# Cross attention in a decoder step: three heads' softmax ahead of the sample rows', two PSUM banks in turn for the heads' logits, and other banks for the first feed-forward block

## The chip, the core and the metric

The kernel runs on one core of a Trainium2 chip. The metric is the device time of one execution in microseconds (us); the time before is the median of three runs. Five engines work side by side, each through a queue of its own in a fixed order: TensorE (PE, with its weight loads as PEld), VectorE (DVE), ScalarE (ACT), GpSimd (POOL) and SyncE (SP), which issues most DMA transfers. An instruction that waits for a semaphore holds up everything that is queued behind it on its engine.

## The reference, cut to what matters

One layer of a hybrid decoder is computed in fp32 for 256 prompt tokens and 8 sample tokens (T = 264 columns): a mixer of sliding-window attention and a state-space scan, then cross attention into 256 memory tokens, then a feed-forward network with a short convolution. The change lies in the cross attention and in the first block of the feed-forward network:

```python
def cross_attend(x, mem_k, mem_v, g_cross, w_cq, cq_norm_g, w_co):
    q = rms_norm((rms_norm(x, g_cross) @ w_cq).reshape(b, t, MEM_HEADS, MEM_HEAD_DIM), cq_norm_g)
    logits = jnp.einsum('bqhd,bshd->bhqs', q, mem_k) * MEM_HEAD_DIM ** -0.5
    p = jax.nn.softmax(logits, axis=-1)
    o = jnp.einsum('bhqs,bshd->bqhd', p, mem_v)
    return o.reshape(b, t, D_XATTN) @ w_co

def conv_ffn(x, past, g_ffn, w_up, conv_w, conv_b, w_down):
    u, new_past = causal_dwconv(rms_norm(x, g_ffn) @ w_up, past, conv_w, conv_b)
    gate, val = jnp.split(u, 2, axis=-1)
    return (jax.nn.silu(gate) * val) @ w_down, new_past
```

There are 4 heads of 128 channels. The prompt's memory keys and values are computed here from the memory tokens; each sample token has its own cached keys and values, which are loaded.

## The kernel before, in words

**Weights.** A product of full precision is made of three matmuls (mm3, L104 to L106): the activations and the weights are split into a high and a low part. A weight part of 128 x 1024 is loaded on SP's queue (wraw, L83), cast on ACT to its high part (whi, L89), and the rest is made on DVE (wlo, L90); each of the three has 4 buffers. mm3 needs whi and wlo.

**PSUM.** There are eight banks of 128 x 512: three called "mm", two "t", and one each of "s", "x" and "y". A bank can be written anew only when everything that reads it is done.

**Order.** The code is traced in the order of its lines, and a scheduler then sets the order on each engine by a model of the times, with a higher priority for weights and for some evacuations (tc.high_priority), and with tc.issue_after for some groups of matmuls. So the order within an engine is fixed before the kernel runs, and an edit in the order of the code can move instructions that it doesn't touch.

**Cross attention**, from about 540 to 620 us of the profiled execution. The queries and the keys stand in SBUF (qk). Then, in the code's order:

- sample_probs (L1134 to L1172): the logits of the 8 sample rows, 32 matmuls against the loaded keys kt (L1144) into bank x; the rows' scale sst with a sum of squares in bank y (L1154), a square root on ACT (L287, called from rms) and two small DVE instructions (L1157, L1159); a maximum and its scaled negative (L1160, L1161); exp (L1163), reciprocal and scale (L1164, L1165); two transposes (L283) and two copies (L1172).
- probs(h) for each of the 4 heads of the prompt (L1194 to L1214): two pairs of fp32 matmuls for the logits into bank s (L1198; the profile counts four for two instructions), the maximum (L1201), a small multiply (L1202), two exps with their sums (L1206), the reciprocal (L1207), two scales (L1209), four transposes into a bank t (L283) and one copy to SBUF (L1214).
- v_pair(i), twice: the memory values of two heads, by mm3 with weights w_cv into two banks mm; two evacuations by ACT (vp<-mm, L1230).
- sample_out after the first v_pair: 16 matmuls of 128 x 512 into bank x (L1180), four DVE instructions (rs, L1183 and L1185), a transpose into bank y, and two splits (L97) that read it, one for each half of the rows.
- out_head(h) (L1236): two matmul pairs, into bank y for heads 0 and 2 and into bank s for heads 1 and 3, and a split of the result into ohl (L97: a cast on ACT, a subtraction on DVE).
- the output projection with w_co, by mm3 from ohl into two banks mm and two banks t, then x2_ev (L1285), which adds the residual (res) and splits the sum into x2h and x2l.

**The feed-forward network** starts at 619.91 us with proj of L1374: two units of up-projection per block i, in the two banks t or two banks mm in turn; block 0 takes banks mm, as the last steps of the output projection do.

Functions on ACT that need another table (square root, exp, silu) are preceded by an ACT_TABLE_LOAD, which the build puts in where the order on ACT asks for it. The names in the orders below end in the number of the buffer's use: e_7276 is the exp of head 1, e_7258 that of head 0, kt_7217 to kt_7223 are sample keys, y_7481 is the transpose of sample_out, y_7487 and s_7626 are the outputs of heads 0 and 3, sst_7243 is the sample rows' scale.

## Time and profile before

| what | us |
| --- | --- |
| median of three runs | 1385.63 (1385.51 to 1386.66) |
| the profiled execution's own time | 1386.54 |
| its span in the trace | 1384.3 |
| PE busy | 1376.5 (99%) |
| DVE, ACT, POOL busy | 1048.7, 766.1, 94.8 |
| DMA moved | 298.31 MB, 215 GB/s |

The profiled execution is 0.9 us above the median, and 2.24 us of it lie outside the span. A timeline row has start, duration, engine, line and operation, output<-inputs, shapes, how many instructions were put together, and in brackets how long the engine stood idle before and whose end it waited for. PE's instructions overlap, so the gap from start to start is what one costs, and the duration of a row is longer. L1198 x4 stands for one head's logits, L283 x4 for one head's transposes, L1144 x32 for one of the two groups of the sample rows' logits.

### The profile page before, as it was taken

How to read it: one execution, taken by the hardware profiler on the slowest of the kernel's cores; microseconds unless marked ns; L12 is line 12 of the kernel's file. 1: busy time of each engine (PE TensorE's matmuls, PEld its weight loads, DVE VectorE, ACT ScalarE, POOL GpSimd, SP SyncE). 2: the span in 40 equal slices, each digit the busy share in tenths (PEclk: the TensorE clock that was granted, in tenths of full speed). 3: DMA queues.
4: the chain of work that ended last, by engine and by line, in shares of the span. 5: the costliest groups of instructions: out<-in, count | busy, mean ns of one | idle time of the engine just before them, and what ended most of it. 6: DMA issues, size and time to landing. Idle time of an engine off the chain costs nothing.

```text
span 1384.3 us, 28768 instructions
## 1 busy us (share of the span) xinstructions
PE 1376.5 (99%) x11415; PEld 1348.3 (97%) x11415; DVE 1048.7 (76%) x1865; ACT 766.1 (55%) x1261; POOL 94.8 (7%) x286
## 2 busy tenths in 40 slices
PE   9999999999999999999999999999999999999999
PEld 8999999999999999889999999999999999999998
DVE  7979799999987774478777775777577757765655
ACT  7667755556545555476565544554455445543532
POOL 0000011111000000002010000000000000000000
PEclk9999999999999999999999999999999999999999
DMA  7954467777677566766576765676667656655664
GB/s 296 331 163 135 145 209 254 232 245 259 234 220 239 182 240 211 308 219 193 187 256 216 259 210 188 214 255 214 186 214 244 196 185 198 198 183 185 192 188 139
DMA packets 89477, 298.31 MB, mean 215 GB/s; under 512 B 12032, under 2 KB 17152, under 8 KB 88832
## 3 DMA queue, kind: packets, MB, share of 16 engines
q1 hardware_dynamic: 83840, 277.61, 60.6%
q0 software_dynamic: 5504, 18.88, 4.2%
q8 instruction: 89, 1.46, 0.4%
q14 instruction: 44, 0.36, 0.1%
HBM read 280.77 MB, written 16.23 MB: 215 GB/s over the span
## 4 chain that ended last, share of the span: by engine, by line
PE 97%; DMA 1%; DVE 1%; ACT 0%; issue 0%; SPq 0%; ACTq 0%
PE mm L105 21%; PE mm L104 20%; PE mm L106 20%; PE t L105 10%; PE t L106 9%; PE t L104 9%; PE t L245 1%; PE t L283 1%; PE y L830 1%; DMA wraw<-in_w_co_dram 1%; PE y L846 0%; DMA open<-in_open_dram 0%; PE x L283 0%; DVE wlo L90 0%; PE s L245 0%; PE mm L245 0%
## 5 line engine op out<-in xcount | busy, mean ns | idle before, releaser
L89 ACT CAST whi<-wraw 128x1024 fp32r<-128x1024 f32 x440 | 459.5, 1047 | 518.2 <-PE mm L105 278.3
L90 DVE TENSOR_TENSOR wlo<-wraw,whi 128x1024 fp32r<-128x1024 f32 x440 | 540.7, 1231 | 220.8 <-ACT whi L89 214.9
L105 PE MATMUL t<-x2l,whi 128*128 128x264 f32 x704 | 200.6, 285 | 0.0
L105 PE MATMUL mm<-x2l,whi 128*128 128x264 f32 x704 | 200.5, 285 | 0.0
L105 PE MATMUL mm<-hl,whi 128*128 128x264 f32 x704 | 199.6, 285 | 0.0
L106 PE MATMUL t<-x2h,wlo 128*128 128x264 f32 x704 | 199.1, 283 | 0.0
L106 PE MATMUL mm<-x2h,wlo 128*128 128x264 f32 x704 | 198.7, 283 | 0.0
L106 PE MATMUL mm<-hh,wlo 128*128 128x264 f32 x704 | 197.6, 282 | 0.0
L104 PE MATMUL mm<-x2h,whi 128*128 128x264 f32 x704 | 196.5, 279 | 0.4 <-DVE res L1285 0.4
L104 PE MATMUL t<-x2h,whi 128*128 128x264 f32 x704 | 196.4, 279 | 0.0
L104 PE MATMUL mm<-hh,whi 128*128 128x264 f32 x704 | 194.1, 280 | 0.0
L104 PE MATMUL mm<-xh,whi 128*128 128x264 f32 x576 | 163.8, 286 | 0.0
L105 PE MATMUL mm<-xl,whi 128*128 128x264 f32 x576 | 163.5, 285 | 0.0
L106 PE MATMUL mm<-xh,wlo 128*128 128x264 f32 x576 | 162.1, 286 | 0.0
L104 PEld LDWEIGHTS mm<-x2h,whi 128*128 128x128 f32 x704 | 132.3, 188 | 0.6 <-ACT whi L89 0.6
L104 PEld LDWEIGHTS t<-x2h,whi 128*128 128x128 f32 x704 | 132.3, 188 | 0.0
L106 PEld LDWEIGHTS t<-x2h,wlo 128*128 128x128 f32 x704 | 132.1, 188 | 0.0
L106 PEld LDWEIGHTS mm<-x2h,wlo 128*128 128x128 f32 x704 | 132.1, 188 | 0.0
L106 PEld LDWEIGHTS mm<-hh,wlo 128*128 128x128 f32 x704 | 131.9, 188 | 0.0
L105 PEld LDWEIGHTS mm<-hl,whi 128*128 128x128 f32 x704 | 131.7, 187 | 0.0
L105 PEld LDWEIGHTS mm<-x2l,whi 128*128 128x128 f32 x704 | 131.7, 187 | 0.0
L105 PEld LDWEIGHTS t<-x2l,whi 128*128 128x128 f32 x704 | 131.7, 187 | 0.0
(497 smaller groups left out, 2893.8 us busy)
## 6 DMA issues: line engine op xcount, KB each, us to landing
wraw<-in_w_up_dram SPq DMA_DIRECT2D x176, 512.0 KB, 4.4
wraw<-in_w_in_dram SPq DMA_DIRECT2D x96, 512.0 KB, 4.7
wraw<-in_w_dn_dram SPq DMA_DIRECT2D x88, 512.0 KB, 4.4
wraw<-in_w_out_dram SPq DMA_DIRECT2D x48, 512.0 KB, 4.3
h<-in_h_dram POOLq DMA_DIRECT2D x32, 256.0 KB, 4.6
hn<-in_h_dram SPq DMA_DIRECT2D x16, 512.0 KB, 4.8
out_state_s_dram<-hn POOLq DMA_DIRECT2D x16, 512.0 KB, 3.6
e<-dram_la SPq DMA_DIRECT2D x16, 256.0 KB, 4.8
```

Source lines behind the costliest of these rows:

```text
L89: S.copy(out=hi, in_=x)
L90: V.tensor_tensor(out=lo, in0=x, in1=hi.bitcast(F32), op=ALU.subtract)
L104: PE.matmul(out, wh, xh, start=start, stop=False)
L105: PE.matmul(out, wh, xl, start=False, stop=False)
L106: return PE.matmul(out, wl, xh, start=False, stop=stop)
L245: PE.matmul(first[c][:, :T], pre[k // 2][i][:, k % 2, c * 128:(c + 1) * 128], A[k // 8][x][:, k % 8, :], start=k + i + x == 0, stop=k == K ...
L283: return PE.transpose(out, in_, cst[0:k, C_ID:C_ID + k])
L830: PE.matmul(y[o:o + 64, (h // 2) * 128:(h // 2) * 128 + 128], xdt[:, h, :], es[h // 4][:, h % 4, :], start=True, stop=True)
```

## The change

sample_probs is cut into three functions: sample_logits (the matmuls), sample_scale (the sum of squares, the square root and the two multiplies) and sample_probs (maximum to transposes). The calls stand in another order: sample_logits, sample_scale, the last loads of the sample values, probs of heads 0, 1 and 2, sample_probs, probs of head 3. The logits of heads 1 and 3 go to bank y, those of heads 0 and 2 to bank s as before. The first up-projection block takes banks s and x, in place of two banks mm. From L1155 on, lines move by 7, and from L1269 on by 8: L1198 becomes L1205, L1206 becomes L1213, L1214 L1221, L1230 L1237, L1236 L1243, L1374 L1382; L1144 stays.

```diff
-    def sample_probs():
+    def sample_logits():
         lg = psum("x")
...
+        return lg
+
+    def sample_scale():
         p = psum("y")
         PE.matmul(p[:, 0:1], qq.rearrange("p m b -> p (m b)"), ones[:, 0:1], start=True, stop=True)
         st = xp.tile([128, 4], F32, name="sst")
-        fs, mx, den = st[:, 0:1], st[:, 1:2], st[:, 2:3]
+        fs = st[:, 0:1]
         V.tensor_tensor(out=fs, in0=p[:, 0:1], in1=r1s[:, 1:2], op=ALU.mult)
         rms(fs, fs, 128)
         V.tensor_tensor(out=fs, in0=fs, in1=r1s[:, 0:1], op=ALU.mult)
+        return st
+
+    def sample_probs(lg, st):
+        fs, mx, den = st[:, 0:1], st[:, 1:2], st[:, 2:3]
         V.tensor_reduce(out=mx, in_=lg[:, 0:256], op=ALU.max, axis=AX.X)
...
     def probs(h, f):
-        p = psum("s")
+        p = psum("y" if h % 2 else "s")
...
-    sample_probs()
+    lg = sample_logits()
+    sst = sample_scale()
     for b in range(6, 8):
...
-    for h in range(2):
+    for h in range(3):
         probs(h, fq[:, :, h])
-    for h in range(2, 4):
-        probs(h, fq[:, :, h])
+    sample_probs(lg, sst)
+    probs(3, fq[:, :, 3])
...
-            proj([w_up[2 * i], w_up[2 * i + 1]], X2, ev, tag="t" if i % 2 else "mm")
+            proj([w_up[2 * i], w_up[2 * i + 1]], X2, ev, tag=["s", "x"] if i == 0 else "t" if i % 2 else "mm")
```

The edit moves instructions on every engine. Two places matter here. The first is about the second group of the sample rows' logits (574 us in the trace of before).

On ACT, before: from the weight cast whi_7561 (565.26 us), over the square root of the sample rows' scale and the evacuations of the first v_pair (vp), to the exps, with the sample rows' exp (es) ahead of head 0's.

```order
L89 CAST whi_7561<-wraw_7559 128x1024
L287 ACTIVATE sst_7243<-sst_7243,eps_414 128x1
L1230 ACTIVATE vp_6702<-mm_7335,rmc_6139 128x256
L89 CAST whi_7567<-wraw_7565 128x1024
L1230 ACTIVATE vp_6702<-mm_7336,rmc_6139 128x256
L89 CAST whi_7643<-wraw_7641 128x1024
L89 CAST whi_7649<-wraw_7647 128x1024
L1163 ACT_TABLE_LOAD
L1163 ACTIVATE es_7250,sst_7243<-x_7192,sst_7243 128x256
L1206 ACTIVATE e_7269,st_7266<-s_7263,st_7266,fq_7174 128x256 x2
```

There is one table load in it. The same place now, from the same weight cast; e_7258 is head 0's exp, e_7276 head 1's, t_7264 head 0's transposes.

```order
L89 CAST whi_7561<-wraw_7559 128x1024
L1213 ACT_TABLE_LOAD
L1213 ACTIVATE e_7258,st_7255<-s_7252,st_7255,fq_7174 128x256 x2
L287 ACT_TABLE_LOAD
L287 ACTIVATE sst_7243<-sst_7243,eps_414 128x1
L1237 ACTIVATE vp_6702<-mm_7335,rmc_6139 128x256
L89 CAST whi_7567<-wraw_7565 128x1024
L1237 ACTIVATE vp_6702<-mm_7336,rmc_6139 128x256
L1213 ACT_TABLE_LOAD
L1213 ACTIVATE e_7276,st_7273<-y_7270,st_7273,fq_7174 128x256
L1221 COPY vp_6702<-t_7264 128x512
L1213 ACTIVATE e_7276,st_7273<-y_7270,st_7273,fq_7174 128x256
```

Head 0's exps now stand ahead of the square root, so there are three table loads, and the evacuations of the first v_pair and the cast whi_7567 stand between head 0's exps and head 1's.

On PE at the same place, before: the second group of the sample rows' logits (L1144) stands among the matmuls of the second v_pair (mm_7498).

```order
L104 MATMUL mm_7498<-whi_7561,mh1_5570 128x256
L105 MATMUL mm_7498<-wlo_7562,mh1_5570 128x256
L1144 MATMUL x_7192<-kt_7223,pp1_6703 32x256 x4
L1144 MATMUL x_7192<-kt_7217,pp1_6703 32x256 x4
L1144 MATMUL x_7192<-kt_7219,pp1_6703 32x256 x4
L1144 MATMUL x_7192<-kt_7221,pp1_6703 32x256 x4
L106 MATMUL mm_7498<-whi_7561,ml_6279 128x256
```

Of the second v_pair's matmuls, 53 stand ahead of that group. Now, with head 1's transposes (t_7282) and the logits of head 3 (y_7317) behind it:

```order
L106 MATMUL mm_7497<-whi_7507,ml_6128 128x256
L1144 MATMUL x_7192<-kt_7223,pp1_6703 32x256 x4
L1144 MATMUL x_7192<-kt_7217,pp1_6703 32x256 x4
L1144 MATMUL x_7192<-kt_7219,pp1_6703 32x256 x4
L1144 MATMUL x_7192<-kt_7221,pp1_6703 32x256 x4
L283 MATMUL t_7282<-cst_68,e_7276 128x128
L1205 MATMUL y_7317<-qk_6701 128x256 x2
L283 MATMUL t_7282<-cst_68,e_7276 128x128 x3
L104 MATMUL mm_7498<-whi_7507,mh0_5569 128x256
```

Here 33 of the second v_pair's matmuls stand ahead of the group; the logits of heads 1 and 2 and head 0's four transposes (t_7264) have moved ahead of it too.

The second place is the end of cross attention. On PE, before: the rows from head 2's logits (s_7299) to the first matmul of the output projection (mm_7637).

```order
L1198 MATMUL s_7299<-qk_6701 128x256 x2
L283 MATMUL t_7293<-cst_68,e_7287 128x128 x4
L283 MATMUL y_7481<-cst_68,rs_7476 128x128
L1198 MATMUL s_7317<-qk_6701 128x256 x2
L283 MATMUL t_7311<-cst_68,e_7305 128x128 x4
L1236 MATMUL y_7487<-vp_6702 128x256 x2
L1236 MATMUL s_7492<-vp_6702 128x256 x2
L104 MATMUL mm_7637<-ohl_7191,whi_7643 128x264
```

And now, from the second v_pair's last matmul on:

```order
L106 MATMUL mm_7498<-whi_7567,ml_6555 128x256
L1243 MATMUL s_7626<-pp1_6703,vp_6702 128x256
L283 MATMUL y_7481<-cst_68,rs_7476 128x128
L1243 MATMUL s_7626<-pp1_6703,vp_6702 128x256
L1243 MATMUL y_7487<-vp_6702 128x256 x2
L104 MATMUL mm_7637<-ohl_7191,whi_7643 128x264
```

The logits and transposes of the heads have moved up from here, and so has head 1's output (s_7492). Head 3's output (s_7626) stands right behind the second v_pair, and head 0's (y_7487) follows the sample rows' transpose (y_7481), which is in the same bank, with half of s_7626 between them.

On ACT at the same place, now; whi_7719 and whi_7725 are weight casts for w_co, and the two rows with y_7481 are the two splits of the sample rows.

```order
L1237 ACTIVATE vp_6702<-mm_7497,rmc_6139 128x256
L1237 ACTIVATE vp_6702<-mm_7498,rmc_6139 128x256
L97 CAST ohl_7191<-y_7481 128x4x4
L97 CAST ohl_7191<-s_7626 128x256
L89 CAST whi_7719<-wraw_7717 128x1024
L89 CAST whi_7725<-wraw_7723 128x1024
L97 CAST ohl_7191<-y_7481 128x4x4
L97 CAST ohl_7191<-y_7487 128x256
L97 CAST ohl_7191<-y_7621 128x256
```

Before, the two splits of y_7481 stood together (x2 in one row), ahead of every cast for w_co but two; now head 3's cast and two weight casts stand between them. DVE has the same five in the same order:

```order
L97 TENSOR_TENSOR ohl_7191<-y_7481,ohl_7191 128x4x4
L97 TENSOR_TENSOR ohl_7191<-s_7626,ohl_7191 128x256
L90 TENSOR_TENSOR wlo_7720<-wraw_7717,whi_7719 128x1024
L90 TENSOR_TENSOR wlo_7726<-wraw_7723,whi_7725 128x1024
L97 TENSOR_TENSOR ohl_7191<-y_7481,ohl_7191 128x4x4
L97 TENSOR_TENSOR ohl_7191<-y_7487,ohl_7191 128x256
```

The subtraction for the second half of the sample rows, which is the last reader of y_7481, stands behind two subtractions for weights.

## Prediction, made before the run

> **What bounds the kernel now.** I read the page first: is there an engine with nothing to spare? Engine, busy time, share of the span, instructions.

> ```profile
> span 1384.3 us, 28768 instructions
> PE 1376.5 (99%) x11415; PEld 1348.3 (97%) x11415; DVE 1048.7 (76%) x1865; ACT 766.1 (55%) x1261; POOL 94.8 (7%) x286
> ```

> PE is it. An edit that leaves PE's matmuls as they are, as this one does, can gain only where PE stands idle, and loses where it makes PE wait. So the second view is PE's waits, over the whole span (bank and line waited in, what for, total, times, longest); the two rows left out lie in the opening.

> ```profile
> PE s L1198 <- ACT ohl L97: 1.0, 1, 1.0
> PE s L1236 <- ACT e L1206: 0.9, 1, 0.9
> PE y L283 <- DVE rs L1185: 0.6, 1, 0.6
> PE mm L104 <- DVE res L1285: 0.4, 1, 0.4
> ```

> All four lie where the change works, and no wait is listed after the last of them, at the start of the feed-forward stage. From there PE has an unbroken queue, so a shift of this start arrives whole at the end. The third view, PE's timeline, gives what they cost.

> ```profile
> 587.29 0.60 PE L283 MATMUL t<-cst,e 128*128 128x128 f32 x4
> 588.50 0.33 PE L283 MATMUL y<-cst,rs 128*128 128x128 f32 x1 [0.60 <-DVE rs L1185]
> 589.80 1.13 PE L1198 MATMUL s<-qk 128*128 128x256 f32 x4 [0.97 <-ACT ohl L97]
> 590.77 0.60 PE L283 MATMUL t<-cst,e 128*128 128x128 f32 x4
> 591.21 1.03 PE L1236 MATMUL y<-vp 128*128 128x256 f32 x4
> 593.15 1.13 PE L1236 MATMUL s<-vp 128*128 128x256 f32 x4 [0.92 <-ACT e L1206]
> ...
> 619.22 0.28 PE L106 MATMUL mm<-ohl,wlo 128*128 128x264 f32 x1
> 619.91 0.36 PE L104 MATMUL mm<-x2h,whi 128*128 128x264 f32 x1 [0.40 <-DVE res L1285]
> ```

> Start to start, and less what the group takes by itself: four transposes take 590.77 to 591.21 = 0.44, so 587.29 to 588.50 holds 1.21 - 0.44 = 0.77 of loss; one transpose takes a quarter of 0.44, so the next step loses 1.30 - 0.11 = 1.19; a head's output takes 0.86 (its row in the chain of waits, below), so 591.21 to 593.15 loses 1.08; and 619.22 to 619.91 loses 0.69 - 0.12 = 0.57, where 0.12 is the step of the last two opening rows below. Restarted groups run some 0.1 longer (589.80 to 590.77 is 0.97, against 0.86), three of them 0.3. **The change can win 0.77 + 1.19 + 1.08 + 0.57 + 0.3 = 3.9 us at most.**

> **What it removes.** The heads' logits and transposes leave the end of cross attention, so nothing there waits for an exp or for bank s; the block in banks s and x doesn't wait for x2_ev. Both banks were last read in the heads' outputs and in rs, some 25 us earlier. I take the whole 3.9 as gone. What is late next is in the new order.

> **What it adds, first place: head 1's transposes.** PE's queue has them right behind the second group of the sample rows' logits. PE reaches them as follows.

> ```profile
> 568.00 0.28 PE L104 MATMUL mm<-whi,mh 128*128 128x256 f32 x1
> 574.10 1.93 PE L1144 MATMUL x<-kt,pp 128*32 128x256 f32 x32
> ```

> The first row is the second v_pair's first matmul. 53 of them, by the order, fill 6.10 us, 0.115 each. Prices of what has moved, from the chain of waits (start, time on the chain, instructions):

> ```profile
> 574.17 1.86 PE x L1144 x32
> ...
> 590.93 0.45 PE t L283 x4
> 595.09 0.86 PE y L1236 x4
> ```

> Now 33 stand ahead: 568.00 + 33 x 0.115 = 571.8; with two more heads' logits (fp32 matmuls of the same number and size as those of L1236, 2 x 0.86) and head 0's transposes (0.45) 574.0; with the sample group (1.86) PE is there at 575.8.

> ACT gets there later. Its rows of before:

> ```profile
> 565.26 1.05 ACT L89 CAST whi<-wraw 128x1024 fp32r<-128x1024 f32 x1 [1.41 <-PE mm L106]
> 566.58 0.30 ACT L287 ACTIVATE sst<-sst,eps 128x1 f32<-128x1 f32 x1 [0.28 <-DVE sst L1157]
> 567.86 0.47 ACT L1230 ACTIVATE vp<-mm,rmc 128x256 f32<-128x256 f32 x1 [0.98 <-PE mm L106]
> 568.25 1.05 ACT L89 CAST whi<-wraw 128x1024 fp32r<-128x1024 f32 x1
> ...
> 576.80 1.28 ACT L1163 ACT_TABLE_LOAD   x1 [1.98 <-DVE sst L1161]
> ...
> 579.19 0.56 ACT L1206 ACTIVATE e<-s,st,fq 128x256 f32<-128x256 f32 x1
> 579.64 0.20 ACT L1206 ACTIVATION_READ_ACCUMULATOR e<-s,st,fq 128x1 f32 x1
> ...
> 582.91 0.58 ACT L1214 COPY vp<-t 128x512 f32<-128x512 f32 x1
> ```

> Now, in the new order: cast to 566.3; table load 1.28, 567.6; two exps 0.56 + 0.65 (579.19 to 579.84), 568.8; table load 1.28, 570.1; square root 0.30, 570.4; the evacuation, 0.39 to the next start (567.86 to 568.25), 570.8; cast 1.05, 571.8. Then DVE:

> ```profile
> 581.95 0.69 DVE L1201 TENSOR_REDUCE st<-s 128x2 f32<-128x512 f32 x1 [0.81 <-PE s L1198]
> ...
> 584.63 0.17 DVE L1207 RECIPROCAL st<-st 128x2 f32<-128x2 f32 x1 [1.79 <-ACT e L1206]
> 584.83 0.62 DVE L1209 TENSOR_SCALAR e<-e,st 128x256 f32<-128x256 f32 x2
> ```

> Its order has the weight subtraction for that cast (1.2, half of the 2.36 at 600.01 below) ahead of two maxima, which overlap by about 0.1, and a small multiply like the reciprocal: 571.8 + 1.2 + 0.69 + 0.60 + 0.17 = 574.4. The third table load waits for it, as the load at 576.80 stood 1.98 us idle until DVE had the exp's operand: 574.4 + 1.28 = 575.7. Exp, copy, exp each step on by 0.47 to 0.54, the last with its sum 0.65: 577.4. Reciprocal 0.2 and the first of two scales 0.31 (half of 0.62): **577.9, against PE's 575.8: 2.2 us of new wait** with latencies. Queued behind it on PE are head 3's logits, 20 matmuls more and all that follows. If the load doesn't wait for DVE, it runs beside it and the wait is 2.2 - 1.28 = 0.9; with no overlap at all it is 2.6.

> **Second place: the end of cross attention.** Head 3's output now follows the second v_pair's last matmul and needs its evacuation, 0.47 of ACT; the matmuls of the other bank cover a step of it: 0.4 (0.2 to 0.6). Before, sample_out's matmuls stood between.

> Then head 0's output (y_7487) must wait until both splits of y_7481 are done, since it is in the same bank. The second split now stands behind head 3's cast and two weight casts on ACT, and two weight subtractions on DVE. The trace of before has just this sequence, less the split:

> ```profile
> 598.66 0.37 ACT L97 CAST ohl<-s 128x256 fp32r<-128x256 f32 x1 [2.29 <-PE s L1236]
> 598.93 2.95 ACT L89 CAST whi<-wraw 128x1024 fp32r<-128x1024 f32 x3
> 600.01 2.36 DVE L90 TENSOR_TENSOR wlo<-wraw,whi 128x1024 fp32r<-128x1024 f32 x2 [0.52 <-ACT whi L89]
> ```

> From the end of s_7626's matmuls to 602.37 it is 3.71 from the cast's start, plus the split of 128 x 16 on DVE (like the small reciprocal, 0.17), plus two semaphores of about 0.1: **4.05 us of wait** (3.5 if one cast starts early; 4.3). The weights lie loaded in their buffers, so nothing but the order holds them. Behind it on PE stands the whole output projection. Its first matmul needs head 0's cast, 0.37 and latencies: 0.6 (0.4 to 0.8).

> **What costs nothing.** SP's queue has the loads of the last sample values one place earlier among those of w_co; the weights of both are used over 15 us later. POOL's order stays. DVE and ACT are at 76% and 55%, and in the output projection PE comes later to each weight, not earlier. The table loads (three for one) are counted in the first wait, their only place on the path.

> **The sum.** Added: 2.2 + 0.4 + 4.05 + 0.6, and three restarts at 0.1: 7.5. Removed: 3.9. **Net +3.6 us.** It is a difference, so it holds from the profiled execution (1386.54, to 1390.1, the span from 1384.3 to 1387.9) as from the median: **1385.63 + 3.6 = 1389.2**. The bounds all together give 0.9 + 0.2 + 3.5 + 0.4 + 0.3 - 3.9 = +1.4 and 2.6 + 0.6 + 4.3 + 0.8 + 0.3 - 3.9 = +4.7; the forecast's own range is 1388.0 to 1390.3.

> **The rivals.** *ACT keeps ahead of PE (faster).* ACT is idle nearly half of the time (598.66 had stood 2.29 idle), and both new waits are for chains that run through it. If it is 2.2 us earlier at head 1's exps, and through the second split of y_7481 by the end of s_7626, PE finds both done, the two evacuations of 0.4 and 0.6 fall into the same slack, and only the old waits go: 1385.63 - 3.9 = 1381.7. It decides at one point, whether ACT's weight casts run before the rows that they hold up or behind them. Against it: each queue keeps its order, and in it the two casts and the split all stand behind a cast that needs s_7626 itself. Chance 0.10, mostly for a mistake in following eleven steps.

> *One of two waits.* Without the first, +3.6 - 2.3 = +1.3, 1386.9; without the tail, +3.6 - 4.15 = -0.5, 1385.1. The first rests on those eleven steps, the tail on three. Chance 0.21.

> *The clock falls.* The tail's gaps come to some 4 us of a PE that does almost nothing. The opening shows what an idle PE comes back at:

> ```profile
> 1.20 3.44 PE L206 MATMUL x<-acc 128*128 128x264 f32 x8 [1.20 <-DVE eps L279]
> ...
> 5.00 0.42 PE L245 MATMUL mm<-xh,whi 128*128 128x264 f32 x1
> 5.22 0.42 PE L245 MATMUL s<-xh,whi 128*128 128x264 f32 x1
> ...
> 6.59 0.28 PE L245 MATMUL mm<-xh,wlo 128*128 128x264 f32 x1
> 6.71 0.28 PE L245 MATMUL s<-xh,wlo 128*128 128x264 f32 x1
> ```

> Matmuls step by 0.22 first and by 0.12 later. PE began at 1.20, so it may run up to 5.4 us at the lower rate, and lose up to 5.4 x (1 - 0.12 / 0.22) = 2.5; with 2.1 taken the time is 1391.3. Against it: ten microseconds with a quarter of idle time kept a granted clock of 1.00 (behind it the DMA share and GB/s):

> ```profile
> 585.00:595.00 10.00, 7.50 (x49) 5.08 (x42) 5.57 (x20) 4.35 (x14) 0.00 (x0) 1.00 0.02 6
> ```

> Those gaps were of 1 us, not 4. Chance 0.11. [...]

> *Table loads dearer than their row.* The load at 576.80 takes 1.28, and this is what I count. If the 1.98 us of idle time ahead of it were the load's own, and not a wait for DVE, the three loads would add 3 x 1.98 = 5.9 to the first wait: 1395.1. Against it: another load, right behind a weight cast, has no idle time ahead of it.

> ```profile
> 635.54 1.28 ACT L287 ACT_TABLE_LOAD   x1
> ```

> [...] Chance of dearer loads 0.03, above the range.

> That the change doesn't do what it says is excluded by the order.

> **How the numbers follow.** Forecast 0.55, one wait 0.21, clock 0.11, dearer loads 0.03, faster 0.10. What a measurement of this kernel can tell is some 0.2%, 2.8 us: below 1382.9 is faster, above 1388.4 slower. Slower: 0.47 of the forecast's 0.55, the clock's 0.11 and the loads' 0.03, 0.61. Within: the rest 0.08 and 0.21, 0.29. Faster 0.10. The range 1385.0 to 1391.4 takes in the forecast, the one-wait cases and the clock's, and leaves out 0.13.

> **What would show it.** Right: the four old waits gone, a wait of some 2 us at head 1's transposes for DVE's scale, one of some 4 at head 0's output, put down to the split of y_7481 on DVE, a first matmul of the up-projection without idle time, and no wait after it. A table load idle for DVE's small multiply between head 0's and head 1's exps. Wrong: new gaps of less than 4 us in all, a matmul step of 0.22 behind the tail, or a wait in the feed-forward stage.

## The result

The changed kernel takes 1392.60 us (median of 6 runs, 1391.63 to 1394.23), against 1386.19 for the kernel before in the same comparison (6 runs, 1385.51 to 1386.66). The ratio is 1.0048, with a 95% interval of 1.0038 to 1.0059: it is slower, by about 6.4 us. The profiled execution took 1392.06, with a span of 1390.0 (before: 1386.54 and 1384.3, so 5.5 and 5.7 more). The six runs of the changed kernel had mean granted clocks of 0.996 to 0.999; the profiled one, at 0.997, took less than the median, and the two at 0.996 took most, 1393.73 and 1394.23. Slower was forecast, with +3.6 us; the measured time lies above the range's upper end of 1391.4.

PE's waits in the changed kernel, to be set beside the four of before (bank, line, what for; total, times, longest):

```profile
PE y L1243 <- DVE ohl L97: 4.0, 1, 4.0
PE t L283 <- DVE e L1216: 1.9, 1, 1.9
...
PE mm L104 <- ACT ohl L97: 0.5, 1, 0.5
PE s L1243 <- ACT vp L1237: 0.2, 1, 0.2
```

All four old waits are gone, and the four new ones are those of the sum, in their places (the row left out, 1.2 us, lies in the opening, as before). On ACT, around the first place, the table loads stand as the order had them:

```profile
564.77 1.05 ACT L89 CAST whi<-wraw 128x1024 fp32r<-128x1024 f32 x1 [1.41 <-PE mm L106]
565.84 1.28 ACT L1213 ACT_TABLE_LOAD   x1
567.13 0.57 ACT L1213 ACTIVATE e<-s,st,fq 128x256 f32<-128x256 f32 x1
...
573.84 1.28 ACT L1213 ACT_TABLE_LOAD   x1 [2.23 <-DVE st L1209]
575.14 0.56 ACT L1213 ACTIVATE e<-y,st,fq 128x256 f32<-128x256 f32 x1
```

The first load starts 0.02 us after the cast ends and the exp 0.01 after the load; the last one stands idle for DVE's small multiply (st, L1209), as forecast. Now PE's timeline at the two places.

```profile
573.59 1.93 PE L1144 MATMUL x<-kt,pp 128*32 128x256 f32 x32
577.47 0.33 PE L283 MATMUL t<-cst,e 128*128 128x128 f32 x1 [1.95 <-DVE e L1216]
...
592.30 0.70 PE L1243 MATMUL s<-pp,vp 128*128 128x256 f32 x2 [0.22 <-ACT vp L1237]
592.95 0.60 PE L1243 MATMUL s<-pp,vp 128*128 128x256 f32 x2
597.52 2.04 PE L1243 MATMUL y<-vp 128*128 128x256 f32 x4 [3.98 <-DVE ohl L97]
600.03 0.81 PE L104 MATMUL mm<-ohl,whi 128*128 128x264 f32 x2 [0.46 <-ACT ohl L97]
600.63 0.65 PE L104 MATMUL t<-ohl,whi 128*128 128x264 f32 x2
601.07 0.42 PE L104 MATMUL mm<-ohl,whi 128*128 128x264 f32 x1
601.29 1.91 PE L1243 MATMUL y<-pp,vp 128*128 128x256 f32 x4
...
603.72 0.28 PE L105 MATMUL t<-ohl,whi 128*128 128x264 f32 x1
603.85 0.28 PE L106 MATMUL t<-ohl,wlo 128*128 128x264 f32 x1
```

The durations behind the tail wait are new: a head's output of four takes 2.04 and 1.91, where before it took 1.03. From 603.72 on, matmuls step by 0.12 to 0.13 again. The windows of the same stretch show why (length; busy time and count of PE, PEld, DVE, ACT, POOL; then the granted clock, the DMA share and GB/s):

```profile
593.28:596.69 3.41, 0.27 (x2) 0.00 (x0) 2.36 (x4) 2.37 (x5) 0.15 (x4) 1.00 0.95 309
596.69:600.10 3.41, 2.12 (x5) 1.24 (x5) 0.78 (x3) 0.37 (x1) 0.00 (x0) 0.50 1.00 347
600.10:603.51 3.41, 3.41 (x12) 3.05 (x13) 0.33 (x1) 0.27 (x1) 0.00 (x0) 0.50 1.02 419
603.51:606.92 3.41, 3.41 (x30) 3.41 (x30) 0.49 (x2) 1.15 (x2) 0.00 (x0) 1.00 0.93 371
```

During the wait the granted clock falls to one half, and it stays there for two windows of 3.41 us. This was one of the rivals, at a chance of 0.11.

### The profile page after: what moved, and what is told of

Its sections match the earlier page's. It is cut to its first block, busy times and chain, and to the rows that moved or that the text cites. A ratio compares the mean times of both kernels' runs of the same rounds, so it can differ in the third digit from the quotient of the medians.

```text
span 1390.0 us, 28770 instructions
## 1 busy us (share of the span) xinstructions
PE 1378.8 (99%) x11415; PEld 1350.0 (97%) x11415; DVE 1048.1 (75%) x1865; ACT 768.2 (55%) x1263; POOL 96.5 (7%) x286
## 3 DMA queue, kind: packets, MB, share of 16 engines
q8 instruction: 89, 1.46, 0.4%
## 4 chain that ended last, share of the span: by engine, by line
PE 98%; ACT 1%; DVE 1%; issue 0%; ACTq 0%
PE mm L104 20%; PE mm L106 20%; PE mm L105 20%; PE t L106 10%; PE t L104 10%; PE t L105 10%; PE t L245 1%; PE t L283 1%; PE y L830 1%; PE y L846 0%; PE mm L245 0%; PE s L245 0%; PE x L283 0%; PE t L564 0%; PE y L1243 0%
## 5 line engine op out<-in xcount | busy, mean ns | idle before, releaser
L89 ACT CAST whi<-wraw 128x1024 fp32r<-128x1024 f32 x440 | 459.8, 1047 | 516.3 <-PE mm L105 268.3
L90 DVE TENSOR_TENSOR wlo<-wraw,whi 128x1024 fp32r<-128x1024 f32 x440 | 540.6, 1230 | 220.7 <-ACT whi L89 214.5
L104 PE MATMUL t<-x2h,whi 128*128 128x264 f32 x704 | 198.5, 282 | 0.0
L106 PE MATMUL t<-x2h,wlo 128*128 128x264 f32 x704 | 198.4, 282 | 0.0
L106 PE MATMUL mm<-hh,wlo 128*128 128x264 f32 x704 | 197.2, 282 | 0.0
L104 PE MATMUL mm<-hh,whi 128*128 128x264 f32 x704 | 195.6, 282 | 0.0
L104 PE MATMUL mm<-x2h,whi 128*128 128x264 f32 x672 | 189.3, 282 | 0.0
L105 PE MATMUL mm<-x2l,whi 128*128 128x264 f32 x672 | 189.3, 282 | 0.0
L106 PE MATMUL mm<-x2h,wlo 128*128 128x264 f32 x672 | 189.3, 282 | 0.0
L104 PE MATMUL mm<-xh,whi 128*128 128x264 f32 x576 | 163.7, 285 | 0.1
L106 PE MATMUL mm<-xh,wlo 128*128 128x264 f32 x576 | 162.2, 286 | 0.0
L104 PEld LDWEIGHTS t<-x2h,whi 128*128 128x128 f32 x704 | 131.9, 187 | 0.0
L106 PEld LDWEIGHTS t<-x2h,wlo 128*128 128x128 f32 x704 | 131.9, 187 | 0.0
L106 PEld LDWEIGHTS mm<-hh,wlo 128*128 128x128 f32 x704 | 131.6, 187 | 0.0
L104 PEld LDWEIGHTS mm<-hh,whi 128*128 128x128 f32 x704 | 130.8, 187 | 0.0
L104 PEld LDWEIGHTS mm<-x2h,whi 128*128 128x128 f32 x672 | 125.9, 187 | 0.0
L105 PEld LDWEIGHTS mm<-x2l,whi 128*128 128x128 f32 x672 | 125.9, 187 | 0.0
```

The source lines that it names most:

```text
L89: S.copy(out=hi, in_=x)
L90: V.tensor_tensor(out=lo, in0=x, in1=hi.bitcast(F32), op=ALU.subtract)
L104: PE.matmul(out, wh, xh, start=start, stop=False)
L105: PE.matmul(out, wh, xl, start=False, stop=False)
L106: return PE.matmul(out, wl, xh, start=False, stop=stop)
```

## The experiments

Theory A says that the new waits are what the sum has them for, and that what is missing in it is the lower clock behind the tail wait. Theory B is the rival: the clock costs nothing, and the excess lies elsewhere. Times are medians beside runs of the kernel before on the same chip.

**The second split ahead of the weight casts.** One line more, in sample_out of the changed kernel:

```diff
-            split(OH[:, :, cs], OL[:, :, cs], x)
+            with tc.high_priority():
+                split(OH[:, :, cs], OL[:, :, cs], x)
```

> The changed kernel with one thing moved: the second split of the sample rows' transpose (y_7481) stands ahead of the two weight casts on ACT and the two weight subtractions on DVE, and all other rows stay. Theory A (the tail wait is the queueing of that split, and on top of it PE comes out of 4 us of idleness at half its clock): the wait falls from 4.0 to about 1.2 us (head 3's split 0.42 and the small split 0.17 on DVE stay ahead), the granted clock stays at 1.00 behind it, and the time falls by 2.8 + 2.4 = 5.2 us, to about 1387.4. Theory B (the clock costs nothing; the excess over the forecast comes from somewhere else): the time falls by 2.8 alone, to about 1389.8. Theory C (the wait is for something else than the split's place): no change, 1392.6.

Measured: 1388.64 us (before 1386.24; ratio 1.0018, 1.0009 to 1.0027). The wait fell from 3.98 to 1.09, so the place of the split makes the wait, and theory C is out. The time fell by 4.0, between the theories, and the trace tells why: the clock still fell, for one window in place of two.

```profile
595.12 1.10 PE L1244 MATMUL y<-vp 128*128 128x256 f32 x4 [1.09 <-DVE ohl L97]
596.73 0.54 PE L104 MATMUL mm<-ohl,whi 128*128 128x264 f32 x2 [0.51 <-ACT ohl L97]
```

```profile
593.67:597.08 3.41, 1.81 (x9) 1.03 (x7) 2.27 (x5) 2.75 (x6) 0.21 (x4) 1.00 0.99 293
597.08:600.50 3.42, 3.10 (x11) 2.44 (x10) 1.10 (x2) 0.15 (x1) 0.00 (x0) 0.50 0.83 335
600.50:603.91 3.41, 3.41 (x31) 3.41 (x30) 0.43 (x2) 1.27 (x2) 0.00 (x0) 1.00 1.03 420
```

The longest gap was 1.09 us, and PE was busy for 1.81 of the 3.41 us ahead of the fall, 53%. In 6 of the 10 runs the mean clock of the run was 0.999 or less, in 4 it was 1.000. The time went with it: the four at 1.000 took 1387.59 to 1388.44 us, five of the other six 1388.84 to 1389.57 (the sixth 1388.29). So no single long gap was needed. Whether the place of the windows in a run decides it, the runs without a profile can't show.

**The wait filled with work.** The order on ACT and DVE stays; PE gets 30 matmuls that nobody reads.

```diff
             heads = out_head(2 * i + m)
+    pf = psum("x")
+    for n in range(30):
+        with tc.issue_after(marks["oh"].ins):
+            PE.matmul(pf[:, 0:256], mem_hl(0)[0][:, 0:128], mem_hl(0)[0], start=True, stop=True)
```

(marks["oh"] is the last matmul of out_head.)

> The changed kernel with 30 extra fp32r matmuls of 128x128 by 128x256 into the free bank x right behind head 3's output, 30 x 0.115 = 3.45 us, so that they lie inside the tail wait; the order on ACT and DVE is unchanged and nothing reads their result. Theory A: head 0's output starts at about the same time after head 3's as before, but PE has been busy, so the granted clock stays at 1.00 and what follows is not slowed: about 2.4 us less, 1390.2, although PE does more. Theory B: no change, 1392.6, or up to 0.3 later.

Measured: 1390.50 us (ratio 1.0032, 1.0020 to 1.0044), 2.1 less than the changed kernel with more to do; the profiled execution, 1389.75 against 1392.06, 2.3 less. This is the cleanest evidence for theory A: the same waits for the same reasons, but a busy PE.

```profile
597.79 1.10 PE L1243 MATMUL y<-vp 128*128 128x256 f32 x4 [0.39 <-DVE ohl L97]
599.35 0.51 PE L104 MATMUL mm<-ohl,whi 128*128 128x264 f32 x2 [0.46 <-ACT ohl L97]
...
601.54 0.28 PE L106 MATMUL t<-ohl,wlo 128*128 128x264 f32 x1
```

From head 0's output to that last matmul it is 601.54 - 597.79 = 3.75 us here and 603.85 - 597.52 = 6.33 in the changed kernel: **the lower clock costs 2.58 us.** In three of the six runs the mean clock was still 0.999; none of these was profiled, so which wait took it down there was not seen. They took 1390.97 to 1391.68 us, the three at 1.000 took 1389.75 to 1390.03.

**The wait filled in part.** The same with fewer matmuls, to tell theories A1 and A2 on the clock apart.

```diff
-    for n in range(30):
+    for n in range(8):
```

> The changed kernel with 8 extra matmuls in place of 30 at the start of the tail wait, 8 x 0.115 = 0.9 us, which leaves a gap of about 3.0 us without any matmul, less than one window of 3.41 us. Theory A1 (the clock falls when PE was busy for less than some 53% of a free-running window): at every phase of the windows some window has at most 49%, so the clock falls in all runs, and the time stays near the changed kernel's, 1392 to 1392.6. Theory A2 (it falls only when a window holds no work at all): the gap can't hold a window, the clock falls in none, and the time is that of the filled kernel's best runs, 1389.9.

Measured: 1392.54 us (ratio 1.0052, 1.0035 to 1.0069), mean clock 0.996 to 0.999 in all four runs. In the profiled one the gap was 3.03 us, shorter than a window, and the clock fell behind a window with 0.43 us of work; A2 is out.

```profile
574.82:578.23 3.41, 1.46 (x29) 0.64 (x22) 0.59 (x3) 3.40 (x9) 0.00 (x0) 1.00 0.88 277
578.23:581.64 3.41, 3.41 (x26) 3.26 (x27) 2.98 (x7) 1.96 (x4) 0.00 (x0) 1.00 0.43 172
...
595.30:598.71 3.41, 0.43 (x2) 0.44 (x3) 2.44 (x3) 1.38 (x3) 0.00 (x0) 1.00 0.98 312
598.71:602.12 3.41, 2.95 (x11) 2.05 (x10) 0.42 (x1) 0.37 (x1) 0.00 (x0) 0.50 0.97 363
```

But A1, a limit taken from the one window of 1.81 us, isn't right either. The first row is the window of the first wait, on the same grid (six windows of 3.41 before the one that ends in the fall): PE was busy for 1.46 us, 43%, and the clock behind it stayed at 1.00. Its work was all but 0.02 us the 32-wide matmuls of the sample rows' logits: 32 of them take 1.86 us, 0.058 each, where an fp32 matmul of the same 256 columns at full width takes 0.215 (0.86 / 4), nearly four times that. But ordinary matmuls show the same. In the run with the second split moved, PE's work ends in the window from 1382.15 to 1385.56:

```profile
1382.15:1385.56 3.41, 1.52 (x13) 1.31 (x11) 0.86 (x2) 0.00 (x0) 0.00 (x0) 1.00 0.34 117
1385.56:1387.04 1.48, 0.00 (x0) 0.00 (x0) 0.00 (x0) 0.00 (x0) 0.00 (x0) 1.00 0.00 0
```

PE was busy for 1.52 us, 45%, and the clock behind it stayed at 1.00, while it had fallen behind the 53% of the tail in the same run. In the changed kernel's trace it fell behind the window in which PE's work ends, with 1.45 us of it (1385.17 to 1388.58; 0.50 from there on). So PE's busy time in the window alone doesn't tell a fall (1.81 and 1.45 us) from none (1.52 and 1.46); what does was not shown.

**The square root ahead of the exps.** In the changed kernel, rms returns its square root, and the exps of probs are issued after it:

```diff
-        rms(fs, fs, 128)
+        marks["sst"] = rms(fs, fs, 128)
...
-            S.activation(out=e3[:, c, :], in_=s3[:, c, :], func=AF.Exp, scale=f[:, c:c + 1], bias=mx[:, c:c + 1], accum_out=den[:, c:c + 1])
+            with tc.issue_after(marks["sst"].ins):
+                S.activation(out=e3[:, c, :], in_=s3[:, c, :], func=AF.Exp, scale=f[:, c:c + 1], bias=mx[:, c:c + 1], accum_out=den[:, c:c + 1])
```

> The changed kernel with the square root of the sample rows' scale held ahead of the heads' exps on ACT, so that one table load is left of three; with it the order changes at the tail too, where both splits of y_7481 now stand together, ahead of head 3's. Theory A: both waits go (1.95 and 4.0), and with the second one the slow clock; what is left of the new waits is the first evacuation (0.4) and the output projection's start (0.6): before less 3.9 plus about 1.2, 1383.5 (to 1384.3). Theory B (no clock in the cost): the changed kernel less 2.0 and 4.0, 1386.6. Theory D (the first wait comes from DVE's queue, not from the table loads): 1 us or more of the first wait stays, 1384.5 to 1385.5.

Measured: 1386.32 us (ratio 1.0000, 0.9991 to 1.0009), 2.8 above the 1383.5 of theory A. By its time alone the run would fit theory B (1386.6); the trace has to decide. The first wait is gone: PE goes from the sample rows' logits to head 1's transposes without idle time.

```profile
573.24 1.93 PE L1145 MATMUL x<-kt,pp 128*32 128x256 f32 x32
575.11 0.66 PE L283 MATMUL t<-cst,e 128*128 128x128 f32 x4
```

DVE's weight subtraction still stands ahead of the two maxima there, so theory D is out. Two table loads are gone from ACT's way, 2 x 1.28 = 2.56, more than the wait of 2.02. (The copy of head 0's transposes, 0.47, has moved behind head 1's exps too; alone it would have left 1.5 us.) The tail wasn't as expected:

```profile
PE mm L104 <- ACT ohl L97: 1.5, 1, 1.5
...
PE y L1245 <- DVE ohl L97: 0.6, 1, 0.6
```

Head 0's split stands behind the two weight casts, as in the changed kernel; but head 0's output was now done while they ran, and the output projection's first matmul waited 1.5 us for the split, where I had put in 0.6. Behind the window that holds this wait and the 0.6 in bank y the granted clock was one half, for one window:

```profile
591.93:595.34 3.41, 1.26 (x8) 0.79 (x7) 2.71 (x4) 1.72 (x3) 0.00 (x0) 1.00 0.90 330
595.34:598.75 3.41, 3.41 (x12) 3.05 (x13) 0.42 (x1) 0.37 (x1) 0.00 (x0) 0.50 1.03 417
```

Against theory B stands the spread within this run's own ten executions: five had a mean clock of 0.999 and took 1386.60 to 1387.29 us, five had 1.000 and took 1385.52 to 1386.04.

**The casts released later.** The code lets the casts for the output projection's later units go after the split kept in `heads`, that of head 3 (L1310). Before, head 3 came last; in the new order it comes ahead of heads 0 and 2. Beside the square root's edit:

```diff
-            heads = out_head(2 * i + m)
+            heads = out_head(2 * i + m) if 2 * i + m == 0 else (out_head(2 * i + m), heads)[1]
```

> The square root held ahead of the heads' exps as in the run before, and the weight casts of the output projection's later units, which the code releases by head 3's split, released by head 0's split instead; so that split stands ahead of the two casts on ACT and the two subtractions on DVE. In the run before, the projection's first matmul waited 1.5 us for that split. Theory A, with the clock rule that the runs so far suggest (it falls after a free-running window of 3.41 us in which PE was busy for less than some 53%, at any length of a single gap): the 1.5 us fall to 0.5, no window has less than 53% any more, the clock stays at 1.00 in all or nearly all runs, and the time is 1384.5 to 1385. Theory B (the clock falls only by a gap of a whole window): 1.0 less than the run before, 1385.3, and half of the runs with a lower clock as there.

Measured: 1383.71 us (before 1386.04; ratio 0.9983, 0.9974 to 0.9992). The 1.5 fell to 0.5, the 0.6 went too, which I hadn't expected, and the clock was 1.000 in all 11 runs. In cross attention and behind it one wait is left:

```profile
PE mm L104 <- ACT ohl L97: 0.5, 1, 0.5
```

The time lies below both theories' (theory A had 1384.5 to 1385, theory B 1385.3). It is 2.6 less than the run before, or 2.4 with each set beside its own runs of the kernel before; 1.0 + 0.6 are the waits. The clock is the likely rest, by my estimate, since the half of the earlier runs with a mean clock of 0.999 took about 1.2 us more. That no run has a lower clock any more is against theory B. The 53% in theory A's rule is the 1.81 of 3.41 us again; that it is a limit was not shown.

**Head 0's output in bank x.** With both edits:

```diff
-        o = psum("s" if h % 2 else "y")
+        o = psum("x" if h == 0 else "s" if h % 2 else "y")
```

> The same, with head 0's output in bank x, so that it needn't wait for the splits of the sample rows' transpose in bank y; head 2's output moves ahead of the output projection by it. The wait for bank y (0.6) goes and the projection's first wait is covered: 0.6 to 1.1 us less than the run beside it, 1383.6 to 1384.2. Rival: head 3's and head 2's splits now stand behind the weight casts, and the projection waits for them instead, up to 1 us: no gain, 1384.7.

Measured: **1382.49 us (ratio 0.9975, 0.9964 to 0.9986): 3.5 us faster than the kernel before**, 10 faster than the change as it was made, and 1.2 less than the run beside it, a little more than expected. The rival's wait for heads 2 and 3 didn't come. All PE waits of the whole span:

```profile
PE x L206 <- DVE eps L279: 1.2, 1, 1.2
PE y L831 <- ACT hp L849: 0.2, 1, 0.2
```

Neither lies in cross attention or behind it. In the one window from 540 to 620 us PE is busy throughout, at a clock of 1.00:

```profile
540.00:620.00 80.00, 80.00 (x688) 74.13 (x687) 50.96 (x100) 47.68 (x87) 0.21 (x4) 1.00 0.76 273
```

The spans of the two profiled executions differ by 1384.3 - 1380.4 = 3.9 us, the bound that the prediction worked out for what can be gained here; the medians differ by 3.55, so the agreement to a tenth is luck.

**Two parts alone.** Of the kernel before, with only the feed-forward block's banks changed:

```diff
-            proj([w_up[2 * i], w_up[2 * i + 1]], X2, ev, tag="t" if i % 2 else "mm")
+            proj([w_up[2 * i], w_up[2 * i + 1]], X2, ev, tag=["s", "x"] if i == 0 else "t" if i % 2 else "mm")
```

> The kernel before with only the first up-projection block's banks changed to s and x. The wait of 0.57 us and its restart at the start of the feed-forward stage go, all others stay: 0.6 us less than before, 1385.6. Rival: the wait moves to a later evacuation, and the time is that of before, 1386.2.

Measured: 1385.43 us (ratio 0.9995, 0.9986 to 1.0005), which a measurement can't tell from no change. The trace shows the step: the wait of 0.4 at the start of the stage is gone, the three others are as before. And with only the logits of heads 1 and 3 in bank y, in probs:

```diff
-        p = psum("s")
+        p = psum("y" if h % 2 else "s")
```

> The kernel before with only the logits of heads 1 and 3 in bank y; the order of the code, one table load and the feed-forward banks as before. If the wait for bank s was what kept the heads' logits late, its 1.0 us goes and perhaps part of the 0.9 behind it: 1 us less than before, 1385.2. Rival: the sample rows' transpose needs bank y too, and now waits for head 3's exps in its place: 1386.2 or slower.

Measured: 1385.15 us (ratio 0.9994, 0.9985 to 1.0002), which can't be told from no change either. The three waits of 1.0, 0.9 and 0.6 gave way to four, and the 0.4 at the start of the feed-forward stage is gone too:

```profile
PE y L283 <- ACT e L1206: 0.5, 1, 0.5
PE y L1236 <- DVE ohl L97: 0.4, 1, 0.4
PE t L283 <- DVE e L1209: 0.3, 1, 0.3
PE s L1236 <- ACT vp L1214: 0.2, 1, 0.2
```

The sum falls from 2.9 to 1.4 us; the first row is the rival's wait, the sample rows' transpose for head 3's exp, but shorter than what it replaces. Neither bank edit makes a loss by itself: it comes with the new order of the code. That order alone, without the banks, was not run.

## Why the prediction was right or wrong

**What bounds the kernel, and the bound of the gain: right.** PE's four waits were all that could be won, 3.9 us by the rows, and the last version of the experiments, in which none is left, has a span shorter by 3.9 (by the medians 3.55).

**The old waits go: right**, all four, as the list of waits shows.

**First place, 2.2 us: right.** PE came to head 1's transposes at 573.59 + 1.86 = 575.45 (forecast 575.8) and started at 577.47 (577.9): 2.02. That it was the table loads is shown by the run with the square root ahead, where two of the three loads and the wait are gone.

**The first evacuation and the projection's start, 0.4 and 0.6: right.** PE idled 0.22 and 0.46 there, and with the restarts 0.39 and 0.70 (from the filled run, 599.35 - 597.79 - 0.86) are lost.

**The tail wait, 4.05 us: right.** From 592.95 to 597.52 it is 4.57 us, of which the rest of head 3's output takes 0.43: 4.14. Its cause, the split's place, is shown by moving it alone. What I hadn't seen is a reason for the order: the casts are tied to head 3's split in the code, which the new order puts ahead of head 0's. The runs show this for head 0's split, which went ahead of the casts when they were tied to it; for the second split of y_7481 it is not shown. The two semaphores of "about 0.1" were an estimate; they took 0.02 (593.56 to 593.58) and 0.14 us (597.38 to 597.52).

**The sum: wrong by the one term that it left out.** The waits make 2.02 + 0.39 + 4.14 + 0.70 = 7.25, less 3.9 is 3.35, close to the +3.6. The clock adds 2.58, so 5.9 against the 5.7 of the spans and the 6.4 of the medians. I had this as a rival with the right place and nearly the right size (2.1 taken, without a reason, and 2.5 at most), but at a chance of 0.11, so the number and most of the range were without it. The forecast's own range should have begun at 1387.0, by the lower bound of +1.4, and not at 1388.0; this changes nothing here.

**The step that failed is the argument against that rival**: "Those gaps were of 1 us, not 4" was true, and I still took the 1.00 of the stretch from 585 to 595 as evidence. That row averaged over ten microseconds at 75% busy, three windows long. By windows of 3.41 us the kernel before had 1.83 us at its emptiest, 54% (586.63 to 590.04), hardly more than the 1.81 us, 53%, behind which the clock fell in an experiment, and its clock stayed at 1.00. By its timeline no stretch of that length between the opening and the end has less, wherever it begins:

```profile
586.63:590.04 3.41, 1.83 (x10) 1.26 (x9) 2.07 (x9) 1.85 (x6) 0.00 (x0) 1.00 0.00 0
```

Of the kernel before's 57 runs beside the experiments one had a mean clock below 1.000 (0.999). And the gap of 4 us needed no luck: all six runs of the changed kernel had a mean clock of 0.996 to 0.999, although a wholly idle window of 3.41 us fits into the idle 3.98 us at only one placement in six (0.57 of 3.41 us). With a grid of 3.41 us laid over its trace at any offset, the emptiest window is at most 38% busy, and the clock fell behind windows with 0.27, 0.43, 1.26 and 1.81 us of work in the profiled runs, none of them empty.

**The rival of dearer table loads: wrong**, as thought. The loads cost 1.28 each; ACT stood idle for 0.02 and 0.01 us ahead of two of them, and the 2.23 ahead of the third ended with DVE's small multiply.

**Faster, or one wait only: did not happen.** Both waits came at their full size.

## What to carry to other kernels

When an edit lets a full PE idle, look at the granted clock behind the idle time too, and don't judge gap by gap: a wait of 4.1 us was followed by 6.8 us at half the clock here and cost 2.6 us more. Gaps of 0.5 to 1.5 us that together left PE 37% or 53% busy over 3.41 us were followed by 3.4 us at half in the profiled runs, and about half of the runs of those kernels show a lower mean clock; two windows, 43% and 45% busy, were followed by the full clock. A group moved ahead takes its dependents along: look for what the code ties to it (here weight casts released by "the last head"), since in each queue they now stand ahead of work that is due earlier. And before a softmax is moved past a square root, count the table loads in ACT's order: three in place of one made PE wait 2 us here, and holding the exps behind the root got them back.
